# First attention: eight transposed chunks a head split by GpSimd from a copy, and V stored in two layouts

## The chip, the cores and the metric

One core of a Trainium2 chip. The metric is the device time of one execution in microseconds (us). The kernel before was timed three times.

## The reference, cut to what matters

Two transformer blocks on a sequence of 2048 tokens of width 1024, all in fp32. What the change touches is the attention of the first block: twelve heads of 64, keys in three windows (the last 128 positions, every fourth of the last 512, every sixteenth of the last 2048), whose results are merged by a softmax over their log-sums.

```python
q, k, v, g_attn, c_h, c_b, c_c, g_conv = jnp.split(rmsnorm(x, g) @ w_in, cuts, axis=-1)
q, k = rope(q), rope(k)
for window, dilation in ((128, 1), (512, 4), (2048, 16)):
    o_i, lse_i = dilated_window_attn(q, k, v, window, dilation)
    ...
mix_w = softmax(stack(lses), axis=0)
o = sum(mix_w[..., None] * stack(outs))
attn_out = o * silu(g_attn)
```

Behind it come the first block's output projection, and a second block with a Fourier mix, a windowed attention and a mixture of 16 experts.

## The kernel before, in words

The order of the work is written out by hand (`manual_schedule`): every engine runs its instructions in the order in which the code issues them, and waits by semaphores for tiles that others write or still read. Matrix products in fp32 are made from two rounded parts of each operand (fp32r: a high part, made by a copy with rounding, and a low part, the difference). `split` makes them, the high part on ACT (L188), the low part on DVE (L189).

**The V stage** (0 to 171.74 us). For each of 16 blocks of 128 tokens PE makes the 768 columns of V in two halves (`v_mm`, L394), and `v_evict` splits them into the tile `vs`, 128 tokens by 12 heads by two parts of 64, 768 KB. The pool of `vs` holds one such tile. `v_store` (L401) then issues the store to the scratch tensor `s_v` on SP's queue; on the same queue follow the load of a later x block (L338) and, behind block 13, the loads of the next stage's weights (`wraw`, L317). ACT's order at the end of the stage is: split of `wraw`, eviction of block 14, eviction of block 15, split of `wraw`. After the stage other tiles take the memory of `vs`: DVE's memset of `ada` (L244) is the first, and behind it in DVE's order stands the low part `wl` (L189) for which PE's first product of the next stage (L481) waits.

**The first attention** (754.64 to 1166 us). Per head there are 32 score tiles: 16 local ones over adjacent keys and 16 over every fourth key, taken in an order of the queries in which positions of one residue lie together (`order`, L777, makes `q2`). `score` is two products on PE and a reduction to the row maximum on DVE (L798). When all 32 are there, `joint` and `joint2` merge the maxima of both sets; `expo` (L829) takes exponentials and row sums on ACT. The weights are transposed on PE in 20 chunks of up to 512 columns (`tpose`, L856), brought to SBUF by `parts`, and multiplied by V (`products`, L876). For 12 chunks of a head `parts` makes two rounded parts, for the eight in the table `WHOLE` it makes one fp32 copy on ACT ("A") or DVE ("V"), and PE multiplies in fp32. The scores of the next head are issued between the chunks of this one, and its exponentials from chunk 17 on; the products of a chunk are issued two chunks after its transposes. `after1` (L892) and `after2` (L896) evict the output banks; the head's output is stored as 64 partitions by SP (L904) and the other 64 are added to it by a GpSimd DMA, `rest` (L905), issued at chunk 6 of the next head.

V has two layouts there: `v1`, tokens in order, loaded from `s_v` (L759), and `v2`, tokens by residue, which 16 casts of 32 partitions a head on GpSimd make from it (`turn_v`, L765). `total` puts the row sums of the residue set back into token order by 16 GpSimd copies (L839), `total2` at chunk 2 of the next head adds and inverts them on DVE (L845, L846), transposes the result on PE (L848), copies it (L850) and stores it (L851). GpSimd also copies the keys to the upper 64 partitions (`repeat`, L661). In the main loop `k` counts the chunks of a head, `h` the heads.

Of the kernel before, what the change touches and what calls it, by code (L numbers as in the profile page):

```python
# [9 lines left out]
F32 = mybir.dt.float32  # L10
F32R = mybir.dt.float32r
# [3 lines left out]
ALU = mybir.AluOpType  # L15
PSUM = bass.MemoryType.PSUM

S, D = 2048, 1024
NT = 16
KC = 8  # L20
H1 = 12
# [72 lines left out]
def prep(inp):  # L94
# [32 lines left out]
SCRATCH = {  # L127
    "s_q": ([H1, 2, 64, S], F32),
    "s_k": ([H1, 2, 64, S], F32),
    "s_v": ([H1, 128, NT, 128], F32),  # L130
    "s_g": ([6, 128, S], F32),
    "s_t": ([6, 128, S], F32),
    "s_mix": ([2, 128, S], F32),
# [164 lines left out]
def phase_a(tc, A, K):  # L298
    nc = tc.nc
    ident, eps = K["ident"], K["eps"]  # L300
    with ExitStack() as es:
# [23 lines left out]
        with ExitStack() as e1:  # L325
# [72 lines left out]
                split(nc, vs[:, hs, 0, :], vs[:, hs, 1, :], p[:, :384].rearrange("p (h d) -> p h d", d=64))  # L398

            def v_store(t, vs):  # L400
                nc.sync.dma_start(A["s_v"][:, :, t].rearrange("h p d -> p h d"), vs.rearrange("p h a d -> p h (a d)").bitcast(F32))  # L401

            with tc.manual_schedule():
                log_exp_tables(tc)
# [226 lines left out]
class QK:  # L631
# [10 lines left out]
    def open(self):  # L642
        self.add(1)
        with self.tc.using_default_side("right"):
            self.q2p = self.es.enter_context(self.tc.tile_pool(name="q2B", bufs=2, reuse_waits="tile"))

    def close(self):
        self.es.close()
# [9 lines left out]
    def repeat(self, h, n, eng):  # L658

        t = self.T[h][n]  # L660
        eng.tensor_copy(t[64:], t[:64].bitcast(F32))  # L661


# [62 lines left out]
def phase_b(tc, A, K):  # L726
# [5 lines left out]
    with ExitStack() as es:  # L732
# [16 lines left out]
        QKs.open()  # L749
        m1 = cp.tile([128, 256], F32, name="m1")  # L750
        m2 = cp.tile([128, 512], F32, name="m2")
        HD = {}
# [19 lines left out]
        def order(h, c, eng):  # L772

            d = HD[h]
            if c == 0:
                d["q2"] = QKs.q2p.tile([128, S], F32R, name="q2")
            eng.tensor_copy(d["q2"][:, c * 512:(c + 1) * 512].rearrange("p (t i) -> p t i", i=32), cls(d["q"], c))  # L777
# [29 lines left out]
            o = c * 512 + a * 128  # L807
            score(h, d["q2"][:, o:o + 128], [cls(d[k], c, 0, 4 * a + 4) for k in ("ka", "kb")], view2(d, c, a), m2)

        WHOLE = [{k: {"A": nc.scalar.copy, "V": nc.vector.tensor_copy}[e] for k, e in enumerate(w) if e != "H"} for w in ("HAHHAHHHHHAHVHVVHHVA", "VVHAVHVVHHVHHHHHHHHH")]  # L810
        def joint(h):

            d = HD[h]
# [15 lines left out]
            nc.scalar.activation(sv, sv, AF.Exp, bias=d["nm"][:, i:i + 1], scale=-1.0, accum_out=d["den"][:, i:i + 1])  # L829

        def total(h):
            d = HD[h]
            L = d["den"]
            E = st.tile([128, 4, 4], F32, name="E2", bufs=2)
            Lr = L.rearrange("p (g c a) -> p g c a", g=2, c=4)
            copy = (nc.gpsimd if h < H1 - 1 else nc.vector).tensor_copy
            for c in range(4):
                for u in range(4):
                    copy(E[QD[c], u, :], Lr[QD[u], 1, c, :])  # L839
            d["E2"] = E  # L840

        def total2(h):
            L, E = HD[h]["den"], HD[h]["E2"]
            r = st.tile([128, 16], F32, name="r", bufs=2)
            nc.vector.tensor_add(r.rearrange("p (a u) -> p u a", u=4), L[:, :16].rearrange("p (u a) -> p u a", u=4), E)  # L845
            nc.vector.reciprocal(r, r)  # L846
            p = ps_t.tile([128, 512], F32, name="pt")
            nc.tensor.transpose(p[:16, :128], r, ident)  # L848
# [10 lines left out]
        def parts(p, w, k, h):  # L859

            hi = pp.tile([128, 512], F32R, name="ph")
            W = WHOLE[h == H1 - 1]
            if k in W:
                whole = hi.bitcast(F32)
                W[k](whole[:, :w], p[:, :w])
# [13 lines left out]
        def chunks(h, last_T):  # L879
# [59 lines left out]
        with tc.manual_schedule():  # L939
# [17 lines left out]
            for i in range(16):  # L957
                turn_v(0, i)
            EX = exps(0)
            ne = 7  # L960
            for e in EX[:7]:
# [11 lines left out]
            TV = {k: (2 * i, 2 * i + 1) for i, k in enumerate((4, 5, 9, 14, 15, 16, 17, 18))}  # L973
            L10, W10, W11 = (4, 13), (8, 9, 16, 17), (4, 6, 8, 10)
            wo_tile = lambda i: (QKs.q2p if i % 4 == 3 else QKs.P[i // 4]).tile([128, S], F32R, name=("q", "ka", "kb", "q2")[i % 4])
# [5 lines left out]
            for h in range(H1):  # L981
# [23 lines left out]
                for k, (_, bl, mm, aft) in enumerate(ch):  # L1005
                    if more and k == SC + JD:
                        joint2(h + 1)
                        EX2 = exps(h + 1)
                    p, w = tpose(bl)
                    while n < len(nxt) and n * SC < len(nxt) * (k + 1):  # L1010
                        nxt[n]()
                        n += 1
                    j = k + LA
                    need = 2 * j + 3 if j < 7 else 20 + -(-4 * (j - 8) // 3)
                    while ne < min(need, 32):
                        EX[ne]()
                        ne += 1
                        if ne == 32:
                            total(h)
                    if more and j >= 17:  # L1020
                        for e in EX2[ne - 32:2 * (j - 17) + 1]:
                            e()
                            ne += 1
                    pend.append((mm, parts(p, w, k, h), aft))
                    products(2)
                    if k == SC and more:
                        joint(h + 1)
                    if k == 2 and h:
                        total2(h - 1)
                    if k == 6 and h:  # L1030
                        HD[h - 1].pop("rest")()
                    if h + 2 < H1:
                        if k in (7, 8):
                            QKs.repeat(h + 2, ("ka", "kb")[k - 7], nc.gpsimd)
                        if 10 <= k < 14:
                            order(h + 2, k - 10, nc.gpsimd)
                    if more:
                        for i in TV.get(k, ()):
                            turn_v(h + 1, i)
                    if h == H1 - 2:  # L1040
                        if k in L10:
                            i = L10.index(k)
                            if i == 0:
                                T = op.tile([128, S], F32, name="T")
                            for j in range(2):
                                wo.load(OUT[2 * i + j], T[:, j * D:(j + 1) * D])
                        if k in W10:
                            i = W10.index(k)
                            wo.split(OUT[i], wo_tile(i), nc.vector.tensor_copy, nc.gpsimd)
                    if not more:  # L1050
                        if k in W11:
                            i = 4 + W11.index(k)
                            wo.split(OUT[i], wo_tile(i), nc.vector.tensor_copy, nc.vector)
                        if k in MU:
                            out.mul(tl, hl, MU[k], nc.gpsimd)
                        if k >= FB:
                            fill.pop(0)()
                        if k == 10:
                            nc.sync.dma_start(x5[:64], A["s_t"][5, :64, :256])
                        if k == 16:  # L1060
                            total2(h)
                            for e in range(2):
                                nc.sync.dma_start(r5[e * 64:e * 64 + 64], A["s_r"][10 + e:11 + e, :256].to_broadcast([64, 256]))
                            nc.gpsimd.tensor_mul(g5, g5, r5)
# [1504 lines left out]
```

## Time and profile before

| | |
|---|---|
| median of 3 runs | 3295.38 us (3294.24 to 3304.3) |
| profiled execution | 3293.63 us, its span 3291.8 us |
| granted TensorE clock | 0.974 of full speed in the mean |
| PE busy | 3110.4 us, 94% of the span |
| DVE, ACT, GpSimd busy | 61%, 44%, 21% |
| DMA | 556.83 MB, mean 169 GB/s |

Times are of one profiled execution, in microseconds from the start of its span. PE is TensorE's matrix products, DVE VectorE, ACT ScalarE, POOL GpSimd, SP the engine whose queue (SPq) issues most transfers. A line number is that of the kernel's code. In a timeline a row may hold several instructions (xN), and what stands in brackets is the idle time of the engine before the row and what ended it. Spans on POOL are rough.

### The profile page before, as it was taken

The page shows a single profiled execution, that of the slowest core. Times are in us where ns is not written, and L with a number is a line of the kernel's source. Part 1 is how long each engine was busy: PE and PEld are TensorE (multiplying, and loading weights), DVE is VectorE, ACT ScalarE, POOL GpSimd, SP SyncE. Part 2 cuts the span into 40 slices and gives each one's busy share as a digit, 9 for nine tenths or more (in the row PEclk, how much of TensorE's full clock was granted, in tenths as well). Part 3 has the DMA queues.
Part 4 walks back from the last instruction along what each step waited for, and adds up shares of the span by engine and source line. Part 5 has one row for each costly group of instructions (what it writes and reads, how often), then busy time and mean ns, then how long its engine had stood idle before and what let it go on. Part 6 is the DMA issues. An engine that isn't in the chain of part 4 may idle for free. (4 is left out here: it accounts for less than half of the span.)

```text
span 3291.8 us, 49939 instructions
## 1 busy us (share of the span) xinstructions
PE 3110.4 (94%) x19200; PEld 2766.1 (84%) x19200; DVE 2021.7 (61%) x4077; ACT 1437.4 (44%) x3072; POOL 675.4 (21%) x784
## 2 busy tenths in 40 slices
PE   9999999999999889789998999489999999999998
PEld 8988877888888767689986778389999999999997
DVE  5445557627888835547777476755565665565654
ACT  4322211105888723436657332244444444454443
POOL 0022210005566447311121010100110010010010
PEclk9999999999999999899999999789999999999999
DMA  5433357405555478544444765346666556665653
GB/s 167 138 132 122 117 184 233 142 20 143 148 126 142 117 218 232 140 132 154 146 139 153 235 187 175 129 180 212 211 211 213 205 205 212 211 217 206 208 203 102
DMA packets 200885, 556.83 MB, mean 169 GB/s; under 512 B 26512, under 2 KB 119580, under 8 KB 180294
## 3 DMA queue, kind: packets, MB, share of 16 engines
q1 hardware_dynamic: 186902, 499.73, 45.3%
q0 software_dynamic: 13456, 53.37, 7.0%
q8 instruction: 151, 2.47, 0.3%
q14 instruction: 88, 0.72, 0.1%
q10 hardware_dynamic: 288, 0.53, 0.0%
HBM read 425.29 MB, written 130.37 MB: 169 GB/s over the span
## 5 line engine op out<-in xcount | busy, mean ns | idle before, releaser
L2481 PE MATMUL mm<-xh,wh 128*128 128x256 f32 x2048 | 581.9, 284 | 0.2 <-ACT xh L188 0.2
L2481 PE MATMUL mm<-xl,wh 128*128 128x256 f32 x2048 | 580.7, 284 | 0.1
L2481 PE MATMUL mm<-xh,wl 128*128 128x256 f32 x2048 | 580.5, 283 | 0.0
L2475 DVE TENSOR_TENSOR wl<-raw,wh 128x1024 fp32r<-128x1024 f32 x380 | 453.8, 1222 | 177.0 <-ACT wh L2474 177.0
L2481 PEld LDWEIGHTS mm<-xh,wh 128*128 128x128 f32 x2048 | 394.2, 192 | 1.1 <-ACT xh L188 0.4
L2481 PEld LDWEIGHTS mm<-xl,wh 128*128 128x128 f32 x2048 | 394.1, 192 | 1.0 <-DVE xl L189 0.4
L2481 PEld LDWEIGHTS mm<-xh,wl 128*128 128x128 f32 x2048 | 394.1, 192 | 0.0
L2474 ACT CAST wh<-raw 128x1024 fp32r<-128x1024 f32 x384 | 390.1, 1049 | 0.0
L481 PE MATMUL mm<-hH,wl 128*128 128x512 f32 x832 | 325.2, 391 | 1.9 <-DVE wl L189 1.9
L481 PE MATMUL mm<-hH,wh 128*128 128x512 f32 x832 | 325.6, 391 | 0.0
L481 PE MATMUL mm<-hL,wh 128*128 128x512 f32 x832 | 325.4, 391 | 0.0
L2536 POOL DMA_INDIRECT out_dram<-yo,idx x32 | 63.1, 1973 | 750.7 <-DVE yo L2535 583.0
L829 ACT ACTIVATE s<-s,nm 128x256 f32<-128x256 f32 (+3 forms) x384 | 202.1, 531 | 19.5 <-DVE nm L824 19.5
L189 DVE TENSOR_TENSOR pl<-pt,ph 128x512 fp32r<-128x512 f32 (+1 forms) x269 | 176.6, 662 | 48.7 <-ACT ph L188 46.6
L2531 PE MATMUL y<-wh,hh 128*128 128x512 f32 x512 | 204.4, 399 | 0.0
L2531 PE MATMUL y<-wh,hl 128*128 128x512 f32 x512 | 200.1, 391 | 0.0
L2531 PE MATMUL y<-wl,hh 128*128 128x512 f32 x512 | 199.7, 390 | 0.0
L188 ACT CAST ph<-pt 128x512 fp32r<-128x512 f32 (+1 forms) x269 | 149.8, 562 | 110.4 <-PE pt L856 40.9
L481 PEld LDWEIGHTS mm<-hH,wl 128*128 128x128 f32 x832 | 157.2, 189 | 35.2 <-DVE wl L189 2.3
L481 PEld LDWEIGHTS mm<-hH,wh 128*128 128x128 f32 x832 | 157.1, 189 | 35.2 <-issue 1.7
L481 PEld LDWEIGHTS mm<-hL,wh 128*128 128x128 f32 x832 | 157.0, 189 | 32.2
L798 DVE CUSTOM_DVE_ANT_0 s<-ps,m 128x256 f32<-128x256 f32 (+3 forms) x384 | 156.9, 449 | 35.2 <-PE ps L797 33.8
(474 smaller groups left out, 6938.1 us busy)
## 6 DMA issues: line engine op xcount, KB each, us to landing
raw<-in_wg SPq DMA_DIRECT2D x32, 2048.0 KB
raw<-in_wd SPq DMA_DIRECT2D x32, 2048.0 KB
raw<-in_wu SPq DMA_DIRECT2D x31, 2048.0 KB
adaw<-in_wada SPq DMA_DIRECT2D x32, 768.0 KB
x<-in_x SPq DMA_DIRECT2D x32, 512.0 KB
wraw<-in_w1t SPq DMA_DIRECT2D x26, 512.0 KB
s_v<-vs SPq DMA_DIRECT2D x16, 768.0 KB
q<-s_q SPq DMA_DIRECT2D x12, 1024.0 KB
```

What stands on the lines that cost most here:

```text
L188: nc.scalar.copy(hi, src)
L189: (e or nc.vector).tensor_tensor(lo, src, hi.bitcast(F32), op=ALU.subtract)
L481: nc.tensor.matmul(p, a[:, k, :], b[:, k, tk], start=i == 0, stop=i == 3 * KC - 1)
L798: nc.vector.tensor_tensor_reduce(sv, p[:, :w], mask[:, mask.shape[1] - w:], 1.0, TOP, ALU.add, ALU.min, d["nm"][:, i:i + 1])
L829: nc.scalar.activation(sv, sv, AF.Exp, bias=d["nm"][:, i:i + 1], scale=-1.0, accum_out=d["den"][:, i:i + 1])
L2474: nc.scalar.copy(hi[:, c], RAW[i][:, c])
L2475: eng.tensor_tensor(lo[:, c], RAW[i][:, c], hi[:, c].bitcast(F32), op=ALU.subtract)
L2481: nc.tensor.matmul(p, a.rearrange("p (k f) -> p k f", k=KC)[:, k, w0:w0 + 128], b[:, k, :], start=i == 0, stop=i == 3 * KC - 1)
L2531: nc.tensor.matmul(ys[sl][:, cs], a[:, kk, sl * 128:sl * 128 + 128], b[:, k, cs], start=kk == 0 and j == 0, stop=kk == 7 and j == 2)
L2536: nc.gpsimd.indirect_dma_start(out=A["out"], out_offset=bass.IndirectOffsetOnAxis(ap=idx[:, sl:sl + 1], axis=0), in_=y, in_offset=None, co ...
```

## The change

It has four parts. `s_v` gets a second copy of V: behind each block's store, four stores of 32 partitions write the same block in the residue layout, and `load_v` loads both layouts. `turn_v` is gone. In heads 0 to 10 no chunk stays whole: eight of the 20 (k = 1, 3, 5, 7, 10, 13, 16, 18, "P" in `PARTS`) are copied by ACT to the new tile `pw` of four places, and GpSimd makes the high part and the low part from it; the other 12 are split by ACT and DVE. The last head keeps its table. `total` becomes 16 small products on PE for heads 0 to 10, issued at k = 2 of the next head, with `total2` at k = 3 and the new `total3` (transpose, copy, store) at k = 5. The products of a chunk are issued three chunks after it; ACT evicts one output bank in `after1` and DVE three; the key copies come in pieces of 512 at k = 6, 8, 9, 11 and the query order at k = 12, 14, 15, 17.

```diff
-    "s_v": ([H1, 128, NT, 128], F32),
+    "s_v": ([2, H1, 128, NT, 128], F32),
...
             def v_store(t, vs):
-                nc.sync.dma_start(A["s_v"][:, :, t].rearrange("h p d -> p h d"), vs.rearrange("p h a d -> p h (a d)").bitcast(F32))
+
+                src = vs.rearrange("p h a d -> p h (a d)").bitcast(F32)
+                nc.sync.dma_start(A["s_v"][0, :, :, t].rearrange("h p d -> p h d"), src)
+                a, u = divmod(t, 4)
+                for c in range(4):
+                    nc.sync.dma_start(A["s_v"][1, :, u * 32:u * 32 + 32, c * 4 + a].rearrange("h p d -> p h d"), src[c * 32:c * 32 + 32])
...
         def load_v(h):
-            v1, v2 = v1.rearrange("p (t d) -> p t d", d=128), v2.rearrange("p (c a d) -> p c a d", c=4, d=128)
-            nc.sync.dma_start(v1.bitcast(F32), A["s_v"][h])
+            v1, v2 = v1.rearrange("p (t d) -> p t d", d=128), v2.rearrange("p (t d) -> p t d", d=128)
+            for i, v in enumerate((v1, v2)):
+                nc.sync.dma_start(v.bitcast(F32), A["s_v"][i, h])
+            v2 = v2.rearrange("p (c a) d -> p c a d", c=4)
-
-        def turn_v(h, i):
-
-            d, (c, u) = HD[h], divmod(i, 4)
-            nc.gpsimd.tensor_copy(d["v2"][QD[u], c], d["v1"][QD[c], u::4].bitcast(F32))
...
-        WHOLE = [{k: {"A": nc.scalar.copy, "V": nc.vector.tensor_copy}[e] for k, e in enumerate(w) if e != "H"} for w in ("HAHHAHHHHHAHVHVVHHVA", "VVHAVHVVHHVHHHHHHHHH")]
+        PARTS = ("HPHPHPHPHHPHHPHHPHPH", "VVHAVHVVHHVHHHHHHHHH")
...
-            split(nc, hi[:, :w], lo[:, :w], p[:, :w])
+            if how == "P":
+                whole = pw[:, k // 2 % 4, :w]
+                nc.scalar.copy(whole, p[:, :w])
+                nc.gpsimd.tensor_copy(hi[:, :w], whole)
+                nc.gpsimd.tensor_tensor(lo[:, :w], whole, hi.bitcast(F32)[:, :w], op=ALU.subtract)
+            else:
+                split(nc, hi[:, :w], lo[:, :w], p[:, :w])
...
-                (nc.vector.tensor_copy if a == 1 else nc.scalar.copy)(T[:, a * 512:(a + 1) * 512], O.pop(a))
+                (nc.scalar.copy if a == 1 else nc.vector.tensor_copy)(T[:, a * 512:(a + 1) * 512], O.pop(a))
...
-                    products(2)
+                    products(3)
                     if k == SC and more:
                         joint(h + 1)
-                    if k == 2 and h:
-                        total2(h - 1)
+                    if h and k in (2, 3, 5):
+                        (total, total2, None, total3)[k - 2](h - 1)
```

Three places where the order moves. First, ACT in the V stage, evictions of block 13 and block 14, as it was: each first half waits for one transfer (DMAHW, a semaphore of the DMA queues) and for DVE.

```order
L188 CAST vs<-mm 128x6x64 [waits DMAHW7_49,DVE_49]
L188 CAST vs<-mm 128x6x64 [waits PE_49]
L188 CAST hH<-pt 128x4x128 [waits PE_49] x2
L188 CAST wh<-wraw 128x1024 [waits DMAHW1_49]
L188 CAST vs<-mm 128x6x64 [waits DMAHW0_49,DVE_49]
```

And now, at the same place:

```order
L188 CAST vs<-mm 128x6x64 [waits DMAHW2_49,DMAHW3_49,DMAHW1_49,DMAHW7_49,DMAHW0_49,DVE_49]
L188 CAST vs<-mm 128x6x64 [waits PE_49]
L188 CAST hH<-pt 128x4x128 [waits PE_49] x2
L188 CAST wh<-wraw 128x1024 [waits DMAHW1_49]
L188 CAST vs<-mm 128x6x64 [waits DMAHW5_49,DMAHW6_49,DMAHW4_49,DMAHW7_49,DMAHW0_49,DVE_49]
```

The order of the instructions is the same; an eviction now waits for five transfers of the block before it.

Second, GpSimd in one head of the attention, as it was, from the row sums of one head on (`E` their copy, `pl` the tile of `v2`, `q` the ordered queries):

```order
L839 COPY E_9192<-den 32x4 x16
L765 CAST pl<-ph 32x512 x10
L905 DMA s_t<-T 64x2048
L661 CAST ka<-ka 64x2048
L661 CAST kb<-kb 64x2048
L765 CAST pl<-ph 32x512 x2
L777 COPY q_9545<-q 128x512 x4
L765 CAST pl<-ph 32x512 x4
```

And now, from the `rest` transfer at chunk 6 to chunk 13 (`ph` and `pl` are here the parts of a chunk):

```order
L921 DMA s_t<-T 64x2048
L667 CAST ka<-ka 64x512 x2
L881 CAST ph<-pw 128x512
L882 TENSOR_TENSOR pl<-pw,ph 128x512
L667 CAST ka<-ka 64x512 x2
L667 CAST kb<-kb 64x512 x2
L881 CAST ph<-pw 128x256
L882 TENSOR_TENSOR pl<-pw,ph 128x256
L667 CAST kb<-kb 64x512 x2
L781 COPY q_7360<-q 128x512
L881 CAST ph<-pw 128x256
L882 TENSOR_TENSOR pl<-pw,ph 128x256
```

The turning casts and the copies of the sums are gone, and each P chunk's two instructions stand between pieces of the copies that were one instruction before.

Third, DVE at the start of a head, as it was: the reciprocal and the copy of its transpose stand together, ahead of a score reduction (L798 ISA, its second row reads the accumulator).

```order
L189 TENSOR_TENSOR pl<-pt,ph 128x512
L845 TENSOR_TENSOR r<-den,E_6366 128x4x4
L846 RECIPROCAL r<-r 128x16
L850 COPY rt<-pt 16x128
L798 ISA s_6447,nm<-ps,m_5772 128x512
```

And now:

```order
L189 TENSOR_TENSOR pl<-pt,ph 128x512
L912 TENSOR_TENSOR T<-po,T 128x16x32
L802 ISA s_6506,nm<-ps,m_5839 128x512
L802 ISA nm 128x1
L802 ISA s_6506,nm<-ps,m_5839 128x128
L802 ISA nm 128x1
L853 TENSOR_TENSOR r<-den,pt 128x4x4
L854 RECIPROCAL r<-r 128x16
```

The sum and the reciprocal stand one chunk later, and the copy of the transpose (now L860) two chunks behind them, among the reductions of chunk 5.

## Rows read from the trace of the kernel before

**Rows 1.** Busy by stage: stretch, us, engines' busy us, PE clock, DMA share, GB/s.
```profile
0.00:171.74 171.74, 164.90 (x941) 156.09 (x942) 80.70 (x176) 67.86 (x145) 4.75 (x8) 0.98 0.51 157
...
754.64:1166.00 411.36, 382.51 (x2933) 337.69 (x2934) 337.43 (x1121) 313.34 (x1002) 246.05 (x460) 0.98 0.51 138
```

**Rows 2.** Timeline of SP's issue queue, V stage: start, us of issuing, instruction.
```profile
34.27 0.39 SPq L401 DMA_DIRECT2D s_v<-vs  x1
...
40.64 0.38 SPq L401 DMA_DIRECT2D s_v<-vs  x1
...
55.52 0.38 SPq L401 DMA_DIRECT2D s_v<-vs  x1
...
64.73 0.38 SPq L401 DMA_DIRECT2D s_v<-vs  x1
...
147.59 0.38 SPq L401 DMA_DIRECT2D s_v<-vs  x1
...
158.56 6.90 SPq L401 DMA_DIRECT2D s_v<-vs  x2
```

**Rows 3.** Timeline of ACT, V stage: start, us, instruction, idle before and releaser.
```profile
39.07 0.86 ACT L188 CAST vs<-mm 128x384 fp32r<-128x384 f32 x2 [1.73 <-DMA s_v<-vs]
...
162.78 0.48 ACT L188 CAST vs<-mm 128x384 fp32r<-128x384 f32 x1 [5.68 <-DMA s_v<-vs]
163.99 0.48 ACT L188 CAST vs<-mm 128x384 fp32r<-128x384 f32 x1 [0.72 <-PE mm L394]
```

**Rows 4.** Timeline of DVE at the V stage's end.
```profile
170.29 0.06 DVE L244 MEMSET ada<- 128x1 f32 x1 [5.23 <-DMA s_v<-vs]
```

**Rows 5.** Timeline of PE at the V stage's end.
```profile
171.74 0.50 PE L481 MATMUL mm<-hH,wl 128*128 128x512 f32 x1 [1.89 <-DVE wl L189]
```

**Rows 6.** Busy by stretch: a V store alone, key loads, 128-partition loads.
```profile
159.50:161.50 2.00, 2.00 (x13) 2.00 (x12) 0.00 (x0) 0.00 (x0) 0.00 (x0) 1.00 1.02 288
799.00:803.00 4.00, 4.00 (x27) 3.20 (x26) 2.95 (x7) 3.56 (x13) 3.28 (x18) 1.00 1.05 213
804.00:808.00 4.00, 4.00 (x28) 3.54 (x28) 3.41 (x13) 2.77 (x9) 2.34 (x4) 1.00 1.02 418
```

**Rows 7.** Busy by stretch: one head of the first attention.
```profile
844.42:874.91 30.49, 29.17 (x240) 26.18 (x238) 26.09 (x90) 25.62 (x84) 19.33 (x40) 1.00 0.53 140
```

**Rows 8.** Waits of PE in eight heads, 813.92 to 1059.06 us.
```profile
PE pt L848 <- DVE r L846: 11.1, 8, 1.6
```

**Rows 9.** Timeline of PE, chunks of one head.
```profile
919.08 0.40 PE L876 MATMUL po<-ph,pl 128*128 128x512 f32 x1
...
919.55 0.60 PE L856 MATMUL pt<-ident,s 128*128 128x128 f32 x4
...
920.95 0.44 PE L818 MATMUL ps<-nm,ident 128*32 128x8 f32 x32
921.31 0.66 PE L856 MATMUL pt<-ident,s 128*128 128x128 f32 x4
...
922.27 1.02 PE L876 MATMUL po<-ph,pl 128*128 128x512 f32 x2
923.13 0.60 PE L856 MATMUL pt<-ident,s 128*128 128x128 f32 x4
```

**Rows 10.** Busy by stretch: chunks 14 of a head to 1 of the next.
```profile
922.05:931.15 9.10, 9.01 (x59) 7.40 (x57) 7.58 (x21) 7.62 (x27) 3.83 (x8) 1.00 0.93 293
```

**Rows 11.** Groups by shape, eight heads: instruction, busy us, mean ns, idle before.
```profile
L765 POOL CAST pl<-ph 32x512 fp32r<-32x512 f32 x128 | 77.5, 606 | 54.3 <-DMA ph<-s_v 41.8 <-PE pt L848 6.5
...
L189 DVE TENSOR_TENSOR pl<-pt,ph 128x512 fp32r<-128x512 f32 x80 | 55.0, 688 | 7.7 <-ACT ph L188 7.3
...
L188 ACT CAST ph<-pt 128x512 fp32r<-128x512 f32 x80 | 46.3, 579 | 16.7 <-PE pt L856 16.7
...
L777 POOL CAST q<-q 128x512 fp32r<-128x512 f32 x32 | 18.3, 609 | 0.5
```

**Rows 12.** Groups by shape, GpSimd, 760 to 1650 us.
```profile
L708 POOL TENSOR_TENSOR g<-g,r 128x512 f32<-128x512 f32 x21 | 27.5, 1308 | 9.6 <-DMA r<-s_r 9.6
```

More of the change, by code (lines that the diff above doesn't have):

```diff
@@ L644, in open @@
         with self.tc.using_default_side("right"):
-            self.q2p = self.es.enter_context(self.tc.tile_pool(name="q2B", bufs=2, reuse_waits="tile"))
+            self.q2p, self.pwp = (self.es.enter_context(self.tc.tile_pool(name=n, bufs=1, reuse_waits="tile")) for n in ("q2B", "pwB"))
     def close(self):
@@ L656, in load, with repeat @@
         self.T[h] = dict(q=q, ka=ka, kb=kb)
-    def repeat(self, h, n, eng):
-        t = self.T[h][n]
+    def repeat(self, h, n, eng, i=None):
+        cs = slice(0, S) if i is None else slice(i * 512, i * 512 + 512)
+        t = self.T[h][n][:, cs]
         eng.tensor_copy(t[64:], t[:64].bitcast(F32))
@@ L751, in phase_b @@
         m2 = cp.tile([128, 512], F32, name="m2")
+        pw = QKs.pwp.tile([128, 4, 512], F32, name="pw")
         HD = {}
@@ L832, in total, with total3 @@
             d = HD[h]
[L833 to L836, printed above, removed]
+            Lr = d["den"].rearrange("p (g c a) -> p g c a", g=2, c=4)
+            if h < H1 - 1:
+                d["E2"] = E = ps_t.tile([128, 512], F32, name="pt")[:, :16].rearrange("p (u a) -> p u a", u=4)
+                put = lambda o, u, x: nc.tensor.matmul(o, ident[:, QD[u]], x, start=True, stop=True, skip_group_check=True)
+            else:
+                d["E2"] = E = st.tile([128, 4, 4], F32, name="E2", bufs=1)
+                put = lambda o, u, x: nc.vector.tensor_copy(o, x[QD[u]])
             for c in range(4):
                 for u in range(4):
-                    copy(E[QD[c], u, :], Lr[QD[u], 1, c, :])
-            d["E2"] = E
+                    put(E[QD[c], u, :], u, Lr[:, 1, c, :])
         def total2(h):
             L, E = HD[h]["den"], HD[h]["E2"]
-            r = st.tile([128, 16], F32, name="r", bufs=2)
+            HD[h]["r"] = r = st.tile([128, 16], F32, name="r", bufs=2)
             nc.vector.tensor_add(r.rearrange("p (a u) -> p u a", u=4), L[:, :16].rearrange("p (u a) -> p u a", u=4), E)
             nc.vector.reciprocal(r, r)
+        def total3(h):
             p = ps_t.tile([128, 512], F32, name="pt")
-            nc.tensor.transpose(p[:16, :128], r, ident)
+            nc.tensor.transpose(p[:16, :128], HD[h].pop("r"), ident)
             rt = st.tile([16, 128], F32, name="rt", bufs=1)
@@ L861, in parts @@
             hi = pp.tile([128, 512], F32R, name="ph")
-            W = WHOLE[h == H1 - 1]
-            if k in W:
+            how = PARTS[h == H1 - 1][k]
+            if how in "AV":
                 whole = hi.bitcast(F32)
-                W[k](whole[:, :w], p[:, :w])
+                {"A": nc.scalar.copy, "V": nc.vector.tensor_copy}[how](whole[:, :w], p[:, :w])
                 return whole,
             lo = pp.tile([128, 512], F32R, name="pl")
-            split(nc, hi[:, :w], lo[:, :w], p[:, :w])
+            if how == "P":
[3 more added lines that the diff above has]
+                nc.gpsimd.tensor_tensor(lo[:, :w], whole, hi.bitcast(F32)[:, :w], op=ALU.subtract)
+            else:
+                split(nc, hi[:, :w], lo[:, :w], p[:, :w])
             return hi, lo
@@ L956, in phase_b @@
                 order(1, c, nc.gpsimd)
-            for i in range(16):
-                turn_v(0, i)
             EX = exps(0)
@@ L972, in phase_b @@
             LA, SC, JD = 1, 14, 1
-            TV = {k: (2 * i, 2 * i + 1) for i, k in enumerate((4, 5, 9, 14, 15, 16, 17, 18))}
+            KD = {k: 2 * i for i, k in enumerate((6, 8, 9, 11))}
+            QO = {12: 0, 14: 1, 15: 2, 17: 3}
             L10, W10, W11 = (4, 13), (8, 9, 16, 17), (4, 6, 8, 10)
-            wo_tile = lambda i: (QKs.q2p if i % 4 == 3 else QKs.P[i // 4]).tile([128, S], F32R, name=("q", "ka", "kb", "q2")[i % 4])
+            wo_tile = lambda i: (QKs.P[i // 4] if i % 4 < 3 else (QKs.q2p, QKs.pwp)[i // 4]).tile([128, S], F32R, name=("q", "ka", "kb", ("q2", "pw")[i // 4])[i % 4])
             T = None
@@ L1017, in phase_b @@
                         ne += 1
-                        if ne == 32:
+                        if ne == 32 and not more:
                             total(h)
@@ L1032, in phase_b @@
                     if h + 2 < H1:
[L1033 to L1039, printed above, removed]
+                        for i in range(KD.get(k, 8), KD.get(k, 8) + 2):
+                            if i < 8:
+                                QKs.repeat(h + 2, ("ka", "kb")[i // 4], nc.gpsimd, i % 4)
+                        if k in QO:
+                            order(h + 2, QO[k], nc.gpsimd)
                     if h == H1 - 2:
@@ L1061, in phase_b @@
                             total2(h)
+                            total3(h)
                             for e in range(2):
```

## The prediction

> **What bounds the kernel now.** First the busy time by stage. In the whole run PE is busy 94% of the span, and the two stages that the change edits differ in how much room they leave [rows 1]: in 0 to 171.74 us, where the V projection runs (the V stage), PE is busy 164.90 of 171.74 us; in the first attention, 754.64 to 1166 us, 382.51 of 411.36. PE work taken off the attention is therefore a gain only while no other engine takes over, and a delay in the V stage is a loss as soon as PE's buffers run dry, since the stages behind it are PE's own and give nothing back.
>
> Second, the issue queue of the V stage [rows 2]. The stores of V follow one another after 6.37 us at first (34.27 to 40.64) and after 9.21 us later (55.52 to 64.73). The first figure is a chain: there is one tile `vs`, so block t+1 may be evicted only when block t's store has landed, and ACT is seen waiting for exactly that at 39.07 and, at the end of the stage, at 162.78 [rows 3]. From the issue at 34.27 to the eviction at 39.07 are 4.80 us, from the eviction to the next issue 1.57 more. The second figure is PE's: a block's products take 9.21 us, and the chain of 6.37 hides under them. The stage's end hangs on the chain again. The last store's landing holds DVE at 170.29, since the memory of `vs` is reused there [rows 4]; DVE's next split waits behind it, and PE for that split until 171.74 [rows 5].
>
> Third, one head of the attention, 30.49 us long [rows 7]: PE 29.17, DVE 26.09, ACT 25.62, GpSimd 19.33. PE has one gap a head, at the transpose of the reciprocal (L848), 11.1 us in eight heads, 1.39 each [rows 8].
>
> **The loss: five stores for one.** Each block's store is followed by four stores of 32 partitions with the same 786,432 bytes together, from the same `vs`; the next eviction waits for all five. Call what they add to a block Q. The trace of before has no transfer of 32 partitions. Rows near it [rows 6]: while a V store runs alone, all 16 DMA engines are full and move 288 GB/s; the 64-partition loads of the keys move 213 GB/s with the engines full too; 128-partition loads move 418. So narrow transfers here go at half the rate of wide ones although no engine is idle. Three values for Q: 786,432 B at 288 GB/s = 2.73 us (width costs nothing), at 213 = 3.7, at 144 (half of the V store's own rate) = 5.46. Less than 2.73 is excluded, since with full engines the bytes can't hide. I take 3.7: the quarter stores are narrow, and of the narrow rows it is the only measured one.
>
> A rule bears on this and speaks against the change. The Trainium skill, "SBUF — State Buffer", section "Door 1: The DMA port swizzle", says that 32 partitions reach 8 of 16 ports, as 64 do, and gives 189 GB/s measured for 1 MiB from partitions 0 to 31. By that figure Q would be an estimated 4.2 us; the rate of 213 on 64 partitions agrees with its halving, and no row here shows 32.
>
> With Q the chain takes 6.37 + Q a block, 10.07 at 3.7: now longer than PE's 9.21, so it sets the stage's pace. Step by step: store 13 is issued at 34.27 + 13 × (6.37 + Q) (before: 147.59, paced by PE). Store 14 follows 10.97 + Q later: 158.56 − 147.59 [rows 2], in which ACT first splits a weight tile whose load stands behind the stores on SP. Store 15 follows 5.80 + Q later: the row of the two stores ends at 165.46, one issue takes 0.38, so store 15 went out at 165.08, 6.52 after store 14; 0.72 of it ACT waited for PE [rows 3], which will be far ahead. PE's next product follows 171.74 − 165.08 = 6.66 us later, plus Q. Sum: 140.5 + 16 Q against 171.74, a loss of 16 Q − 31.2. **Q 2.73 gives +12.4, 3.7 gives +28, 5.46 gives +56.** The 31.2 is the room that PE's pace hid so far. By the page's figure the stage would lose an estimated 36 us. The four more issues a block, 0.38 each on SP, lie beside the transfers, and the x loads behind them are two blocks early.
>
> **The gain: PE's side of a head.** A whole chunk (fp32) costs PE more than two rounded parts [rows 9]: 512 columns 0.86 us (922.27 to 923.13) against 0.47 (919.08 to 919.55). Eight whole chunks a head become parts, five of 512 columns, one of 384, two of 256. The pieces into which a chunk's columns are cut change the saving a little; read from start to start in the same way, k = 1, 4, 10, 12, 14, 15, 18, 19 save 0.24, 0.375, 0.19, 0.345, 0.39, 0.345, 0.345, 0.19: 2.42 us. The gap of 1.39 (1.32 in the head read) goes, as the transpose moves from k = 2 to k = 5 and its reciprocal stands at k = 3. The sums of `total` are 16 small products on PE instead of GpSimd copies: 32 like ones take 0.36 (920.95 to 921.31), so at most +0.37. PE alone would need 30.5 − 3.4 = **27.1 us a head**.
>
> **What takes over.** GpSimd: it loses 16 turning casts of 0.606, 9.7 us, and the small copies, and gets eight copies and eight subtractions over 3200 columns: 6.25 × 0.609 [rows 11] + 6.25 × 1.308, the price of a 512-column two-input operation on GpSimd [rows 12], 12.0 us. At most 21.6 of 27, no bound. A chunk of 512 takes 0.579 on ACT, 0.609 and 1.308 on GpSimd, 2.5 us in a row, and products that come three chunks later leave it about 4.5 (three of twenty chunks of a head). DVE: four copies of 512 columns go (about 0.69 each, as its subtraction of that size [rows 11]), two evictions of the outputs come: about 25. ACT: four more chunk copies of 0.579, two evictions of about as much fewer: 25.6 + 1.1 = 26.8 of 27.1 in the mean, and not evenly. In the stretch from chunk 14 to the next head's chunk 1, PE is busy 9.01 of 9.10 us and ACT 7.62 [rows 10]. There PE loses 0.39 + 0.345 + 0.345 + 0.19 + 0.24 = 1.51, and ACT gains three chunk copies that DVE made (14, 15, 18; 0.485 slot each), about 1.5: PE wants 7.6, ACT 9.1. So ACT paces the tail, and the 1.5 saved there is not got. DVE's low part of the last chunk then waits for ACT's high part, 0.69 [rows 11], ahead of the next head's score reductions, for which PE waits. I take 3.4 − 1.5 − 0.7 = **1.2 us a head** with bounds 0 and 3.4. For eleven heads −13. Against it +2.5: the second V layout is another 1 MB load, 2.5 us at 418 GB/s, ahead of the `rest` transfer, on whose landing the output weights' loads wait in head 10, where nothing hides it. In other heads that load hides: DMA is at half its capacity. The attention gives about **−10**.
>
> **Sum.** 3293.63 (profiled execution, 1.75 below the median of 3295.38) + 28 − 10 = 3312. A measurement here can tell about 0.3%, 10 us, so this is slower.
>
> **Rivals.** (a) Width costs nothing: Q = 2.73, +12.4 − 10, 3296, no change. For it: the V store itself already runs at 288 rather than 418, so its small packets may be the limit at any width. Against it: 213 on the half-width loads. (b) Both limits multiply: Q = 5.46, +56 − 10, 3340. (c) The other side, faster: ACT runs ahead through the tail, so each of eleven heads gives the full 3.4, −37, and a loss of 12 to 28 remains under it: 3269 to 3285. The place is ACT's queue from chunk 14 on; it decides when ACT enters the tail 1.5 us or more ahead of PE. For it: ACT's mean still fits below PE's. Against it: its order is fixed and the exponentials it could do early wait for the joint maxima at the same point. By (c) the whole is faster only if Q stays under 3.5. (d) The attention gives nothing or loses, with Q 3.7: 3322 or more.
>
> **Chances.** Forecast with its neighbours, Q 3.2 to 4.6 and an attention of −3 to −20: 0.50, slower but for 0.03. (a) 0.18, of which 0.16 no change and 0.02 faster; (b) 0.12; (c) 0.12, of which 0.09 faster; (d) 0.08. So faster 0.11, same 0.22, slower 0.67. The range leaves out the extremes of (b) and (c): 3282 to 3342.
>
> **What would show it.** In the profile after: V stores with intervals of about 10 us from the first to the last, ACT idle before each eviction for a transfer of `vs`, PE idle for buffers in the V stage, its first product of the next stage at about 200 us rather than 171.74. A head of about 29.3 us, without the gap at the transpose, with PE waiting for ACT between chunk 14 and the next head's start. Wrong if the stores keep 9.2 us, or if heads fall to 27.

## The result

The changed kernel takes 3340.3 us (median of 4 runs, 3332.04 to 3345.36) against 3294.81: ratio 1.0131, 95% interval 1.0100 to 1.0162. The forecast was 3312 with a range of 3282 to 3342. The profiled execution has a span of 3341.4 us, 49.6 more than the one before. Where they come from, by the start of the same PE instruction in both traces (lag: how much later it starts after the change):

| place | before | after | lag | added there |
|---|---|---|---|---|
| PE's first product that waits for the V stage's end | 171.74 | 205.60 | +33.9 | 33.9 |
| first attention starts | 754.64 | 793.29 | +38.7 | 4.8 |
| merge of the maxima in head 9 (for head 10) | 1074.55 | 1108.34 | +33.8 | -4.9 |
| the same in head 10 | 1107.79 | 1145.21 | +37.4 | 3.6 |
| last transposes of the attention | 1155.69 | 1201.17 | +45.5 | 8.1 |
| output projection, last products | 1354.07 | 1403.12 | +49.0 | 3.6 |

The V stage first. SP's issue queue, where four narrow stores (L406) now follow each wide one (L403), and the last regular store:

```profile
33.21 0.39 SPq L403 DMA_DIRECT2D s_v<-vs  x1
33.65 4.93 SPq L406 DMA_DIRECT2D s_v<-vs  x4
...
44.10 0.38 SPq L403 DMA_DIRECT2D s_v<-vs  x1
```

```profile
170.57 0.38 SPq L403 DMA_DIRECT2D s_v<-vs  x1
```

From the first store to the fourteenth are 137.36 us, 10.57 a block; before, PE's 9.21 paced it [rows 2]. PE, which was busy without a gap from 40 to 160 us, is busy 111.85 of these 120 us now. Four narrow issues hold SP for 4.93 us, where a wide one takes 0.39. ACT in the same stage (start, duration, instruction, idle time and what ended it):

```profile
42.54 0.86 ACT L188 CAST vs<-mm 128x384 fp32r<-128x384 f32 x2 [6.26 <-DMA s_v<-vs]
...
182.08 1.04 ACT L188 CAST wh<-wraw 128x1024 fp32r<-128x1024 f32 x1 [11.23 <-DMA wraw<-in_w1t]
...
193.83 0.86 ACT L188 CAST vs<-mm 128x384 fp32r<-128x384 f32 x2 [9.95 <-DMA s_v<-vs]
```

ACT's wait for the stores at the start has grown from 1.73 to 6.26 us, at the end from 5.68 to 9.95 [rows 3]. DVE and PE at the end of the stage:

```profile
204.16 0.06 DVE L244 MEMSET ada<- 128x1 f32 x1 [8.80 <-DMA s_v<-vs]
```

```profile
205.60 0.80 PE L486 MATMUL mm<-hH,wl 128*128 128x512 f32 x1 [9.17 <-DVE wl L189]
```

The chain of [rows 4, 5] is the same, each link longer. Busy time by stretch (length, then busy PE, PEld (TensorE's loads of weights), DVE, ACT, POOL, granted clock, DMA share, GB/s): a wide store, narrow stores, and three stretches after PE's restart.

```profile
98.50:100.50 2.00, 2.00 (x13) 2.00 (x12) 1.39 (x6) 0.53 (x3) 0.00 (x0) 1.00 1.02 290
101.50:103.00 1.50, 1.50 (x14) 1.46 (x13) 0.00 (x0) 0.00 (x0) 0.00 (x0) 1.00 0.96 163
205.60:208.00 2.40, 2.40 (x6) 1.92 (x7) 0.00 (x0) 0.15 (x1) 0.00 (x0) 0.50 0.98 403
208.00:212.00 4.00, 4.00 (x14) 3.19 (x13) 0.00 (x0) 0.21 (x1) 0.93 (x1) 0.70 0.99 392
212.00:216.00 4.00, 4.00 (x19) 3.28 (x19) 1.49 (x3) 0.60 (x1) 1.66 (x2) 1.00 0.06 24
```

The narrow stores move 163 GB/s with the DMA engines about as full (0.96) as at 290. And PE, idle for 9.17 us before 205.60, restarts at a granted clock of 0.50, the 1.2 GHz level, and is at 2.4 GHz again by 212: the lag grows there from 33.9 to 36.1 us.

One head of the attention by stretch, and PE in it (timeline):

```profile
897.26:927.41 30.15, 28.59 (x272) 26.39 (x271) 24.81 (x89) 26.57 (x86) 20.24 (x30) 1.00 0.60 176
```

```profile
902.51 0.66 PE L866 MATMUL pt<-ident,s 128*128 128x128 f32 x4 [0.52 <-DVE pl L189]
...
905.76 0.50 PE L801 MATMUL ps<-ka,q 128*128 128x512 f32 x1 [0.98 <-DVE nm L802]
...
908.58 0.88 PE L842 MATMUL pt<-den,ident 128*32 128x4 f32 x32
909.38 0.66 PE L866 MATMUL pt<-ident,s 128*128 128x128 f32 x4
```

A head is 30.15 us; between the same two points it was 30.63 (859.68 to 890.31). The gap at the transpose of the reciprocal [rows 8] is gone. In its place stand two waits, 0.52 and 0.98 us, and the small products of `total`, 0.8 us (908.58 to 909.38).

### The profile page after: what moved, and what is told of

It reads as the page before. It is cut to its first block, busy times and chain, and to the rows that moved or that the text cites. A ratio compares the mean times of both kernels' runs of the same rounds, so it can differ in the third digit from the quotient of the medians.

```text
span 3341.4 us, 50718 instructions
## 1 busy us (share of the span) xinstructions
PE 3121.9 (93%) x19552; PEld 2775.5 (83%) x19552; DVE 2011.3 (60%) x4057; ACT 1441.1 (43%) x3092; POOL 672.9 (20%) x652
```

## The experiments

The theory: the five stores through the one tile `vs` make the V stage late because the narrow ones are slow; the attention gains little because ACT paces the end of a head. Rivals stand in the expectations. The measured time of a head is the distance from one merge of the maxima to the next, in heads 2 to 9.

**One store.** The four narrow stores are left out, both loads read the first copy.

```diff
-                for c in range(4):
-                    nc.sync.dma_start(A["s_v"][1, :, u * 32:u * 32 + 32, c * 4 + a].rearrange("h p d -> p h d"), src[c * 32:c * 32 + 32])
...
-                nc.sync.dma_start(v.bitcast(F32), A["s_v"][i, h])
+                nc.sync.dma_start(v.bitcast(F32), A["s_v"][0, h])
```

> The four 32-partition stores a block are left out and the attention loads the first layout for both sets, so the residue set multiplies V rows in the wrong order; the work of all engines is otherwise that of the changed kernel. Theory (the five-store chain through the one tile vs sets the V stage's pace): the stores are 9.2 us apart again, PE's first product behind the V stage falls back from 205.6 to about 172 us and the attention starts at about 755 instead of 793; 3340 - 38 = 3302 us. What is left over the kernel before, some 8 us, is then the attention and what lies behind it. Rival (the stage is late for another reason, or the delay is given back later anyway): above 3325.

Measured: 3297.21 us, ratio to before 1.0009 (1.0000 to 1.0018); attention starts at 752.22; head 30.16. The attention starts 41 us earlier than in the changed kernel and the run is 43 us shorter: the narrow stores are the loss. What the heads gain is given back in this run too: the merge in head 9 comes 6.7 us earlier than before (1067.83 against 1074.55), and the span is 5.1 us longer (3296.9 against 3291.8).

**One wide store in their place.**

```diff
-                for c in range(4):
-                    nc.sync.dma_start(A["s_v"][1, :, u * 32:u * 32 + 32, c * 4 + a].rearrange("h p d -> p h d"), src[c * 32:c * 32 + 32])
+                nc.sync.dma_start(A["s_v"][1, :, :, t].rearrange("h p d -> p h d"), src)
```

> In place of four stores of 32 partitions one store of 128 partitions with the same 786,432 bytes, into the second copy but in the first layout (V rows of the residue set in the wrong order). Theory (width costs the time): the added time a block falls from 4.2 us to about 2.7, the chain to some 9.1 to 9.4 us, which is PE's own pace; stage loss 12 to 16 us instead of 34 to 38, 3314 to 3320 us. Rival (the bytes cost it, whatever the width): 4.2 us a block and 3340. Second rival (a wide store overlaps the first one so that little is added): near 3302 as with one store.

Measured: 3310.83 us, 1.0049 (1.0034 to 1.0064); attention starts at 768.32, +13.7. SP's queue, and PE's restart behind the stage:

```profile
33.25 0.39 SPq L403 DMA_DIRECT2D s_v<-vs  x1
33.69 0.75 SPq L405 DMA_DIRECT2D s_v<-vs  x1
...
42.45 0.36 SPq L403 DMA_DIRECT2D s_v<-vs  x1
```

```profile
183.08 0.79 PE L485 MATMUL mm<-hH,wl 128*128 128x512 f32 x1 [7.73 <-DVE wl L189]
```

9.20 us a block, and PE is busy from 40 to 160 us without a gap. ACT still waits for the stores in each block, so they add some 2.83 us (9.20 less 6.37). Hidden under PE's pace up to the last blocks, they cost 11.3 us at PE's restart (183.08). One store of the same bytes from 128 partitions lets the attention start 25 us earlier than four from 32, and the run is 29 us shorter. So the narrow stores cost by how they are made, not by their bytes. Width and number change together here, one store for four, and no run parts the two; that the DMA engines are full while narrow stores run (a share of 0.96 at 163 GB/s) speaks against a limit in the issuing.

**Narrow stores of the two halves in turn.** `for c in (0, 2, 1, 3)`.

> The four narrow stores in the order of partitions 0, 64, 32, 96 instead of 0, 32, 64, 96; nothing else. Theory (a narrow store is slow because its partitions reach only half of the ways out, and stores of the other half can run beside it): neighbours now use different halves, the added time a block falls to 2.7 to 3.5 us, 3312 to 3328 us. Rival (each narrow store is slow by itself or is issued too slowly, one after the other): still 4.2 us a block, 3340.

Measured: 3337.03 us, 1.0126 (1.0110 to 1.0141).

```profile
34.11 0.39 SPq L403 DMA_DIRECT2D s_v<-vs  x1
34.55 4.67 SPq L406 DMA_DIRECT2D s_v<-vs  x4
...
44.51 0.38 SPq L403 DMA_DIRECT2D s_v<-vs  x1
```

The interval is 10.40 in the mean of thirteen, where the changed kernel has 10.57. The order of the partitions changes little; the theory of the halves in turn falls. Why a narrow store is slow is not settled beyond that.

**Head 10 with the old table.** `PARTS` gets a third entry for head 10, the old string of whole chunks.

> Head 10 alone goes back to the old table of whole chunks (copies by ACT and DVE), heads 0 to 9 stay. Theory (in head 10 the two GpSimd instructions of a chunk stand behind the output weights' subtractions of 2.4 us each on GpSimd, and PE waits for them: 3.9, 0.7 and 3.8 us): about 8 to 11 us less, 3330 us. Rival (head 10 is late because the weights' raw loads land later, behind the second V load): no change, 3340.

Measured: 3337.68 us, 1.0135 (1.0113 to 1.0157), no difference to the changed kernel that shows. PE in head 10 and behind it in the changed kernel, and then in this one:

```profile
1136.51 0.58 PE L801 MATMUL ps<-ka,q 128*128 128x256 f32 x1 [3.83 <-DVE nm L802]
...
1155.80 0.65 PE L892 MATMUL po<-ph,pl 128*128 128x384 f32 x1 [3.89 <-POOL ph L881]
1157.15 0.69 PE L892 MATMUL po<-pl 128*128 128x384 f32 x1 [0.70 <-POOL pl L882]
```

```profile
1138.50 0.38 PE L801 MATMUL ps<-ka,q 128*128 128x256 f32 x1 [3.17 <-DVE nm L802]
...
1141.54 0.58 PE L801 MATMUL ps<-ka,q 128*128 128x256 f32 x1 [0.91 <-DVE nm L802]
...
1156.38 0.55 PE L866 MATMUL pt<-ident,s 128*128 128x128 f32 x3 [1.55 <-DVE ph L875]
...
1177.02 0.93 PE L722 MATMUL mm<-kb,ph 128*128 128x512 f32 x2 [3.97 <-ACT ph L188]
```

The waits for GpSimd (L892 <- POOL) are gone, others stand there. From the merge of the maxima that opens head 10's stretch to the first load of the output weights (T<-in_wo) are 23.6 us in the changed kernel (1108.34 to 1131.95), 23.5 here, and 19.2 before (1074.55 to 1093.79). So the half of the rival is borne out that says late loads: they wait for `rest`, and are some 4 us later in the head. The other half, that they stand behind the second V load, is not. SP's queue before, and in the changed kernel (the store of the head's output is L904, now L920):

```profile
1083.89 0.47 SPq L904 DMA_DIRECT2D s_t<-T  x1
...
1093.79 12.41 SPq L675 DMA_DIRECT2D T<-in_wo  x4
```

```profile
1119.76 0.32 SPq L767 DMA_DIRECT2D pl<-s_v  x1
1121.36 0.47 SPq L920 DMA_DIRECT2D s_t<-T  x1
1131.95 0.81 SPq L681 DMA_DIRECT2D T<-in_wo  x2
```

The store of the head's output, for which `rest` waits, went out 9.34 us after the merge before and goes out 13.02 after it now, 13.02 in this run too. That is 3.7 of the 4.4 us. The store goes out when DVE has evicted the last output bank (L912, 1120.62 to 1121.30), and not when the V load (L767) lets it. The order issues a chunk's products one chunk later than before; how much of the 3.7 that is, was not tried, and neither was moving the loads alone.

**`total` on GpSimd.** The copies come back, the sum at chunk 5 and the transpose at 7.

```diff
-                put = lambda o, u, x: nc.tensor.matmul(o, ident[:, QD[u]], x, start=True, stop=True, skip_group_check=True)
+                put = lambda o, u, x: nc.gpsimd.tensor_copy(o, x[QD[u]])
...
-                        (total, total2, None, total3)[k - 2](h - 1)
+                        {2: total, 5: total2, 7: total3}[k](h - 1)
```

> The sixteen small products of `total` go back to GpSimd copies (still issued at chunk 2; the sum and reciprocal move to chunk 5 and the transpose to chunk 7 so that nothing waits for them there). Theory (the small products cost PE 0.9 us a head, not 0.37, and that is a part of why a head is 30.16 us): head period 29.3 to 29.7 us. Rival (the head is paced by ACT and DVE through the tail, PE's 0.9 only fills a wait): 30.1 us. Second rival (GpSimd, 2.9 us fuller, becomes late for the chunks at 3 and 5): 31 us or more.

Measured: one run of 3331.81 us; a head takes 29.51, 0.65 less. Its stretch:

```profile
898.25:927.77 29.52, 27.95 (x239) 25.59 (x238) 24.95 (x89) 26.73 (x86) 23.08 (x46) 1.00 0.61 180
```

PE is busy 27.95 instead of 28.59; the two waits are unchanged. The theory holds.

**Copies of chunks 16 and 18 on DVE.**

```diff
-                nc.scalar.copy(whole, p[:, :w])
+                (nc.vector.tensor_copy if k in (16, 18) else nc.scalar.copy)(whole, p[:, :w])
```

> The copies from PSUM of chunks 16 and 18 are made by DVE instead of ACT; GpSimd's part stays. Theory (ACT paces chunks 14 to 19 and DVE waits for its high parts, which gives PE's two waits of 0.52 and 0.98 us a head): the waits shrink or go, head period 28.7 to 29.4 us. Rival (DVE is the one that is late there, by the score reductions and output evictions): the waits grow, 30.5 us or more. Second rival (PE's wait at the score products comes from the exponentials' buffers and neither engine's copies): 30.16 as now.

Measured: one run of 3336.27 us; a head takes 29.40, 0.76 less, and PE's two waits shrink:

```profile
934.78 0.66 PE L866 MATMUL pt<-ident,s 128*128 128x128 f32 x4 [0.33 <-DVE pl L189]
...
937.55 0.50 PE L801 MATMUL ps<-ka,q 128*128 128x512 f32 x1 [0.50 <-DVE nm L802]
```

ACT was the late engine in the tail.

**Whole chunks in all heads.** Heads 0 to 10 get the old string.

> Heads 0 to 10 go back to the old table of eight whole chunks a head (four copies by ACT, four by DVE); second V layout, `total` on PE and the products three chunks late stay. GpSimd has then only key copies and query order. Theory (the tail took back what the parts save on PE, and the head's gain of 0.47 is the old gap of 1.39 less the 0.9 of `total`): about 30.1 to 30.3 us a head, that is no slower than the changed kernel's 30.16. Rival (the parts do gain 1.2 or more a head and something else was lost): 31 us or more.

Measured: one run of 3344.89 us; a head takes 29.99, less than with parts:

```profile
901.38:931.37 29.99, 29.99 (x271) 26.95 (x270) 26.83 (x93) 24.88 (x83) 7.61 (x13) 1.00 0.60 178
```

PE is busy all the time, and still the head is 0.17 us shorter. So the eight chunks that GpSimd splits gained nothing in the changed kernel. Without them a head takes 0.64 us less than before (30.63), which is about the old gap of 1.32 less the price of `total`, 0.65 by the run that moved it.

**The second layout from memory to memory**, 64 transfers behind the V stage, with head 10 as above.

```diff
+            def turn():
+                t = TC.pop(0)
+                a, u = divmod(t, 4)
+                for c in range(4):
+                    nc.sync.dma_start(A["s_v"][1, :, u * 32:u * 32 + 32, c * 4 + a], A["s_v"][0, :, c * 32:c * 32 + 32, t])
...
                             rope(*last)
+                            if TC and n % 3:
+                                turn()
```

> The second layout is not stored from the tile vs; 64 transfers from the first copy to the second, memory to memory, are spread over the projections behind the V stage, where DMA is at 0.39 of its capacity; and head 10 uses the old table. Theory: V stage as before (attention starts at 752 to 756 us), heads 30.16, the total 3294 to 3297 us, no different from the kernel before. Rival (the transfers hold up weight loads and rope stores on the same queue, so the projections are late): 3305 or more.

Measured: 3334.39 us, 1.0125 (1.0108 to 1.0142): the rival. The V stage is as before, but the attention starts at 785.29. SP's queue:

```profile
248.67 10.46 SPq L521 DMA_DIRECT2D s_v<-s_v  x4
...
284.88 0.52 SPq L513 DMA_DIRECT2D s_q<-hi  x1
288.29 0.52 SPq L513 DMA_DIRECT2D s_q<-lo  x1
288.86 6.15 SPq L521 DMA_DIRECT2D s_v<-s_v  x4
```

SP is held up to 10 us by four of them, and the rope stores behind them (rotated queries and keys, `s_q<-hi`, `s_q<-lo`) are late: ACT's waits for the rope stores of the high parts (`s_q<-hi`, `s_k<-hi`) come to 142 us between the V stage and the attention, where they were 69 before. By themselves the rope stores move 102 GB/s at a DMA share of 0.26, before as in this run. Three stretches: rope stores in the kernel before, rope stores in this run, and the last of the transfers from memory to memory, behind which SP issues nothing else until they are done:

```profile
234.00:240.00 6.00, 6.00 (x28) 4.99 (x27) 3.97 (x3) 2.03 (x4) 2.98 (x2) 1.00 0.26 102
```

```profile
286.00:288.00 2.00, 1.66 (x7) 1.39 (x8) 1.21 (x1) 0.78 (x2) 1.58 (x2) 1.00 0.26 102
711.00:717.00 6.00, 6.00 (x28) 4.96 (x27) 0.00 (x0) 0.59 (x1) 0.00 (x0) 1.00 0.88 162
```

So the transfers from memory to memory move 162 GB/s with the DMA engines nearly full.

**The second layout made by the load.** Two versions. In the first the load gathers 512-byte pieces whose outermost index has four values.

```diff
+            for c in range(4):
+                nc.sync.dma_start(v2[:, c * 4:c * 4 + 4].bitcast(F32), A["s_v"][0, h, c * 32:c * 32 + 32].rearrange("i (a u) d -> u i a d", u=4))
```

> One layout is stored, by the one wide store a block; the second is made by the load: four transfers a head, each 128 partitions, 256 KB in pieces of 512 bytes, read V in the residue order. With it `total` on GpSimd (as in the run that moved it), the copies of chunks 16 and 18 on DVE, head 10 with the old table. Theory (the loss is the chain through vs alone, the two head edits add up): V stage as before, attention starts at 752 to 755 us, heads 28.6 to 28.9 us (30.16 - 0.65 - 0.76), less some 8 us given back at head 10 to the output projection: 3278 to 3286 us, faster than the kernel before by 0.25 to 0.5%. Rival (the gathered loads are slow and late, 1 MB in 512-byte pieces while keys and queries load): heads 30 us or more, 3295 or more.

> The same V stage and loads, `total` on GpSimd, but heads 0 to 10 with the old table of whole chunks, so that GpSimd makes no parts. Theory (what the parts are worth once the tail is balanced is small): heads 29.99 - 0.65 to 0.9 = 29.1 to 29.35, 3283 to 3290 us, some 4 to 7 us behind the run with parts. Rival (the parts are worth nothing even then): no difference to that run. Second rival (they are worth the full 2 us a head): 20 us behind it.

Measured: with parts 3428.76 us, 1.0392 (1.0377 to 1.0408); with whole chunks 3318.2, 1.0067 (1.0054 to 1.0081). A stretch in which SP issues these loads:

```profile
872.00:880.00 8.00, 8.00 (x63) 7.46 (x62) 7.54 (x29) 7.57 (x25) 4.11 (x6) 1.00 0.28 76
```

76 GB/s at a DMA share of 0.28, about 4 of 16 engines. (The Trainium skill, "DMA: Bandwidth & Descriptors", section "Why a DMA increments its semaphore by 16 and not by 1", says that the sizes of the slowest dimension on both sides set how many engines a transfer uses; this share agrees.) The head's output store stands behind them on SP, `rest` waits for it on GpSimd, and the parts queue behind `rest`: PE waits 9 us a head for a high part, which the run without parts is spared. That run loses its time at both ends: from merge to merge its first step takes 47.7 us and the one to head 10's merge 48.1, where they were 28.2 and 33.2 before. The pattern was mine and the theory was not tested by it.

In the second version blocks are stored in another order, so that a piece is 2 KB and the outermost index has 32 values, and the loads stand behind the output store.

```diff
-                nc.sync.dma_start(A["s_v"][0, :, :, t].rearrange("h p d -> p h d"), src)
+                nc.sync.dma_start(A["s_v"][0, :, :, t % 4 * 4 + t // 4].rearrange("h p d -> p h d"), src)
...
+        def load_v2(h):
+            for u in range(4):
+                nc.sync.dma_start(HD[h]["v2"][QD[u]].rearrange("i c a d -> i c (a d)").bitcast(F32),
+                                  A["s_v"][0, h, :, u * 4:u * 4 + 4].rearrange("(c i) a d -> i c (a d)", i=32))
...
+                    if k == 3 and more:
+                        load_v2(h + 1)
```

> One wide store a block, with the blocks in another order in memory, so that the residue layout can be loaded by four transfers of 32 partitions a head in pieces of 2 KB; they are issued at chunk 3, behind the head's output store on SP. `total` on GpSimd, copies of chunks 16 and 18 on DVE, head 10 with the old table. Theory (as for the run that gathered with one slow pattern; that pattern, which moved only some 76 GB/s, is gone): V stage as before, heads 28.6 to 28.9 us, less some 8 us given back at head 10 and in the output projection: 3278 to 3287 us, faster than the kernel before by 0.25 to 0.5%. Rival (narrow loads of 1 MB a head hold up the next head's keys or the rest transfer): heads 30 us or more, 3295 or more.

> The same stores, loads and `total`, but heads 0 to 10 with the old table of whole chunks. Theory: heads 29.1 to 29.35 us, 3283 to 3291 us, 4 to 7 us behind the run with parts. Rival: no difference to that run, so the parts are worth nothing even with the tail balanced. Second rival: 20 us behind it, so they are worth the full 2 us a head.

Measured: with parts 3288.04 us, 0.9973 (0.9962 to 0.9984); with whole chunks 3287.59, 0.9976 (0.9967 to 0.9986). Both beat the kernel before and the changed one. One head of each, with parts and without:

```profile
911.17:939.94 28.77, 27.90 (x239) 25.56 (x238) 25.86 (x91) 26.07 (x84) 23.01 (x46) 1.00 0.72 185
```

```profile
916.38:945.47 29.09, 29.09 (x239) 26.26 (x239) 26.68 (x93) 24.87 (x83) 10.44 (x29) 1.00 0.69 182
```

28.77 against 29.09 us a head: with the tail balanced the parts are worth 0.32 us a head, some 3 us of the run, which the two totals can't tell apart. The rival of no difference between the two holds as far as the totals go. Some 8.5 us of what the heads gain in the run with parts (the merge in head 9 is 19.55 us earlier than before, the one in head 10 only 14.87, the output projection's last products 11.0) are given back from head 10 on.

## Why the prediction held in sign and missed in size

The sign, the place and the order of the steps were right; the median lies 1.7 us inside the range. That it lies there is luck in part: the upper end stood for rival (b), whose mechanism did not happen. The two terms of the sum were both too kind. Against them the output projection's last products are some 31 us later than forecast: 5.9 in the V stage (33.9 where 28 were forecast), 4.8 between PE's restart and the attention, 8.1 in the heads up to the merge in head 9 (a gain of 4.9 where 13 were forecast for all eleven), 9.2 from there to the attention's end (a loss of 11.7 where 2.5 were forecast), and 3.6 in the output projection.

- **Q.** I took 3.7 us from the 64-partition loads; the intervals give 10.57 - 6.37 = 4.20. With 4.2 the chain's formula gives +36 at PE's restart; measured are +33.9, and half of the difference is that the first store went out at 33.21 instead of 34.27. The Trainium skill, "SBUF — State Buffer", section "Door 1: The DMA port swizzle", has 189 GB/s for 32 partitions, by which an estimated 4.2 was given: the runs agree (786,432 bytes in 4.20 us are 187 GB/s). That was the figure to take.
- **What follows the restart** was not in the sum: 2.2 us at the lower clock, and 4 us more at the first product that makes the modulations (L290), where PE waits for ACT's split of its operand; 1.4 of these come back before the attention. PE's row there, before and after:

```profile
463.89 0.34 PE L290 MATMUL adap<-adah,adao 128*1 128x384 f32 x1 [3.99 <-ACT adah L188]
```

```profile
503.95 0.48 PE L290 MATMUL adap<-adah,adao 128*1 128x384 f32 x1 [7.94 <-ACT adah L188]
```

- **Rival (a)** fell with the interval of 10.57; the wide-store run shows 2.83 where it assumed 2.73, and what it would have cost: +11.3 us at PE's restart against +12.4 worked out. Rival (b) did not happen: 4.2 is far from 5.46; its 3340 was met by what came behind the V stage, not by its mechanism. In the attention it is rival (d) that happened, with Q at 4.2 instead of 3.7, to which I gave 0.08: the lag grows there by 6.8 us, from 38.7 to 45.5, where I had a gain of 10.
- **PE's side of a head.** The forecast wanted 27.1, a saving of 3.4. `total` costs 0.80 on PE, and 0.65 in the time of a head, where I took 0.37 from 32 like products; why these take twice that was not tried. Summed from start to start, with the listed waits taken off, the products with V of one head cost 12.15 us before and 10.10 in the changed kernel (12.02 in the run with all whole): 2.05 saved, where I had 2.42. With the gap of 1.32 PE's own saving is 2.57.
- **The tail.** That ACT paces it was right: the run with two copies on DVE shows it. The 2.2 us a head that I took for it were near: 1.50 of listed waits, and 0.6 by which the scores (10.03 to 10.51) and the transposes (6.65 to 6.76) take longer from start to start; what of that is waiting the trace does not list. 2.57 less 2.09 is the measured 0.48. Rival (c), ACT running ahead, fell.
- **Head 10.** I priced the later weight loads at 2.5 us, for a V load ahead of them. From the merge in head 9 on the attention loses 11.7, and the output projection 3.6 more. I had seen that the loads wait for `rest`, but not that the head's output store, and `rest` with it, comes some 4 us later in the head. The parts of head 10 behind 2.4 us subtractions on GpSimd do not explain the loss: without them the run is no shorter. What share the later loads have is open, as is the output projection's part.

## What to carry to other kernels

A store from a single buffer is part of the loop: what it adds to a block is free only up to the slack between the chain and the engine that paces the stage, here 2.8 us a block, and beyond that every microsecond counts as many times as there are blocks. At the end of the stage nothing hides it: the second wide store, about as long as the slack, still cost 11.3 us at PE's restart. Make a second layout on the side that has slack, and look at how wide each transfer is and how its outermost index spreads. Work taken from a busy engine is worth only as much as its neighbours' order allows: balance the stretch in which the neighbour is already full before adding to it.

## What the runs showed that was not expected

Three kinds of transfers were slow with nothing else in their way: stores from 32 partitions, 187 GB/s in the mean with the engines full; transfers from memory to memory in 512-byte pieces, 162 GB/s at a share of 0.88; loads whose outermost index has four values, 76 GB/s at 0.28. In the last the engines are idle for the most part, and so they are while the rope stores run, 102 GB/s at 0.26. And a narrow store holds SP longer than a wide one: 4.93 us for four against 0.39 for one.
